# The fifth of seven inner products of an MLP's second layer is multiplied by the seven-product scheme once more

## The chip, the core and the metric

The kernel runs on one core of a Trainium2 chip. The metric is the device time of one execution in microseconds (us). The core has TensorE (PE in the profile; its weight loads are PEld), VectorE (DVE), ScalarE (ACT), GpSimd (POOL) and SyncE (SP), which here issues nearly all DMAs. The 16 DMA engines of the core carry every transfer.

## What is computed

One layer of an encoder trunk on one sequence of 2048 rows and 1024 columns: a mixer (two kinds of attention) and then an MLP, both behind a norm with shift and scale. Only the MLP matters here:

```python
h = rmsnorm(x, g_norm2[l]) * (1.0 + sc2) + sh2
x = x + gt2 * (jnp.square(jax.nn.relu(h @ w1[l])) @ w2[l])
```

`w1` is 1024 x 4096 and `w2` 4096 x 1024, all in float32.

## The kernel before

**Three matmuls for one.** Every float32 operand is split into a rounded part and a rest (`split`: ACT casts `hi`, DVE subtracts to get `lo`). `mm3` then makes three matmuls: hi by hi, hi by lo, lo by hi. Each operand of 128 x 512 so costs one ACT cast and one DVE subtraction, and lies in a tile of the pool `opp`, which has eight.

**Seven products for eight.** Both layers of the MLP are cut in 2 x 2 blocks and multiplied by a Strassen scheme in Winograd's form, which needs seven block products (numbered 1 to 7, `OUTER`) in place of eight, for sums and differences of blocks. Each of the seven takes sums of the blocks of one side and of the other. `mb` is the half of the sequence (mb=1 is worked on first, then mb=0), `tb` a block of 512 rows of it, and `odd` says which of the two.

**The first layer** (class `First`) runs 16 groups of seven steps for each half; a step is 12 matmuls. Its outcome, the hidden activations and their sums, goes to DRAM (`scr_hid[mb, i, ...]`, i being the product of the second layer that will use it).

**The second layer** has the same seven products i, of [hidden, 4096 deep] by [w2]. They come in two kinds.
- A *plain* product (class `Second`, list `PLAIN`) runs 16 steps of 12 matmuls, once for each half of the sequence.
- A *doubled* product (class `Outer`, list `DOUBLE`) takes both halves of the sequence as a 2 x 2 block problem again and applies the seven products inside it: seven times eight steps of 6 matmuls, run once, when mb=0's hidden activations are there. It needs sums on both sides: those of the weights are made ahead, during mb=0's first layer (`outer_sums`, one per group of seven steps, stored to `scr_t`); those of the hidden activations are partly made on the fly, where the first layer subtracts the other half's value from what it stores (`First.other` loads it, `First.keep` subtracts), and partly just before the product, as half sums of 128 x 1024 on DVE (`half`, `half_sum`, placed by `plan`).

Before, the products 1, 6 and 5 are plain and 7, 2, 3 and 4 doubled. The order of work is: out projection, first layer of mb=1, plain 1, 6, 5 of mb=1, first layer of mb=0, plain 1, doubled 7, plain 6, doubled 2, plain 5, doubled 3, doubled 4. Within the plain products of mb=1 lies the preparation of mb=0's normed input (`right_blocks`, four times, ten steps apart). The products 1 and 6 (and 5) are summed in four accumulator tiles (`Second.whole`), and `update` adds these sums to rows of x: it loads a row block, adds (`weigh`, DVE), and stores. A doubled product adds its results itself (`load_x` loads the rows, `end` adds).

**Who sets the order.** The MLP is a list `steps`; `at(n, job)` hangs loads and sums on a step. PE and SP keep the order in which the program emits their instructions; ACT and DVE get theirs from the scheduler of the tile framework. Operands are prepared ahead as long as at most eight tiles are ready or in use; a first-layer step uses one, a plain step two, two doubled steps three. A store that waits for DVE holds up all that SP has behind it; a load also waits until its tile is free.

**The pools.** `ring` (three buffers of 8 KB a partition) and `spare` (one) hold the raw weights; `tp` has seven temporary rows of 128 x 512, `accp` twelve such tiles ("kept"), `rp` two, which hold the norm rows that `right_blocks` multiplies by.

Every group of the profile names line 42, a helper that records instructions, so groups are told apart by their tiles: `opr` and `ol` are the two operands of a doubled product, `oph` and `opv` those of a plain one, `opw` and `h` those of the first layer; `r` is a half of hidden activations, `l` and `hw` raw operands, `xo` and `xu` rows to be added to, `wt` raw weights for sums.

## Time and profile before

| | us |
|---|---|
| median of 3 runs | 2551.41 (2550.36 to 2551.88) |
| profiled execution | 2549.72 |
| its span | 2548.0 |
| PE busy | 2520.9 |
| DVE busy | 2010.0 |
| ACT busy | 1498.6 |
| share of the DMA engines of queue q1 | 79.7% |

The span is the time from the first to the last instruction of the profiled execution. Busy times are unions of an engine's instructions. Matmuls overlap their neighbours, so that an unbroken run of them shows as 100% busy; how many of them fit in a stretch tells whether PE ran at its pace.

### The profile page before, as it was taken

To read this page: it belongs to the slowest core of one execution; us is meant where nothing else is said; L and a number is where in the kernel's file an instruction comes from. 1 tells how busy PE (TensorE), PEld (TensorE's weight loads), DVE (VectorE), ACT (ScalarE), POOL (GpSimd) and SP (SyncE) were. 2 spreads that over 40 slices of the span, in tenths; PEclk is the share of its full clock that TensorE was granted. 3 is DMA by queue.
4 is the path that set the end of the run, shared out by engine and by line. 5 is a ranking of instruction groups with operands and counts; after the bars stand their busy time and mean duration, and the time that the engine had idled before them with its cause. 6 is when DMAs were issued, how large, how long until landed. Compare 5 with 4: busy or idle time off the path is not lost.

```text
span 2548.0 us, 39355 instructions
## 1 busy us (share of the span) xinstructions
PE 2520.9 (99%) x12436; PEld 2104.0 (83%) x12436; DVE 2010.0 (79%) x3509; ACT 1498.6 (59%) x2871; POOL 747.0 (29%) x1128
## 2 busy tenths in 40 slices
PE   9999999999999999999999999999999999999999
PEld 7888888888888888887988888888888887888887
DVE  7656767887789878998858777668988766988897
ACT  6333425668866677666755555566555555656565
POOL 4330154776776667776620000000000000000000
PEclk9999999999999999999999999999999999999999
DMA  9879979779987788866787888787899889777772
GB/s 359 327 295 365 348 269 295 216 243 291 284 237 235 239 251 269 268 211 196 230 301 253 301 284 281 257 312 260 279 323 303 264 274 394 273 285 271 281 266 83
DMA packets 293200, 698.92 MB, mean 274 GB/s; under 512 B 31360, under 2 KB 83584, under 8 KB 281856
## 3 DMA queue, kind: packets, MB, share of 16 engines
q1 hardware_dynamic: 291696, 691.69, 79.7%
q10 hardware_dynamic: 1296, 4.72, 0.5%
q8 instruction: 98, 1.61, 0.3%
q14 instruction: 110, 0.90, 0.1%
HBM read 477.66 MB, written 218.63 MB: 273 GB/s over the span
## 4 chain that ended last, share of the span: by engine, by line
PE 83%; DVE 6%; DMA 3%; ACT 3%; issue 2%; POOL 1%; SPq 0%; DVEq 0%; ACTq 0%; POOLq 0%
PE ps L42 27%; PE ps_s L42 14%; PE pt L42 11%; PE acc L42 6%; PE wt L42 6%; PE pf L42 4%; PE z L42 4%; PE po L42 4%; PE pq L42 3%; DVE p L42 2%; PE cz L42 2%; DMA hw<-in_w_dram 1%; PE ct L42 1%; DVE opr L42 1%; ACT z L42 1%
## 5 line engine op out<-in xcount | busy, mean ns | idle before, releaser
L42 PE MATMUL ps<-h,opw 128*128 128x512 f32 x1512 | 358.6, 389 | 0.0
L42 ACT CAST wth<-wt 128x512 fp32r<-128x512 f32 (+3 forms) x544 | 257.3, 484 | 166.0 <-PE wt L42 156.9
L42 POOL TENSOR_TENSOR b<-p 128x512 f32<-128x512 f32 (+1 forms) x320 | 292.5, 914 | 168.0 <-DVE p L42 95.0
L42 DVE TENSOR_TENSOR wtl<-wt,wth 128x512 fp32r<-128x512 f32 (+3 forms) x544 | 291.2, 547 | 57.6 <-ACT wth L42 55.8
L42 PEld LDWEIGHTS ps<-h,opw 128*128 128x128 f32 x1512 | 283.7, 188 | 58.8
L42 PE MATMUL pt<-w,ht 128*128 128x512 f32 x1248 | 288.2, 391 | 0.0
L42 PE MATMUL ps_s<-h,opw 128*128 128x512 f32 x1152 | 277.3, 389 | 0.4 <-ACT ps_s L42 0.4
L42 PEld LDWEIGHTS pt<-w,ht 128*128 128x128 f32 x1248 | 232.9, 188 | 47.7
L42 DVE TENSOR_TENSOR_SCAN p<-z,p,zero 128x512 f32<-128x512 f32 x192 | 245.8, 1281 | 25.7 <-ACT z L42 18.1
L42 PE MATMUL ps<-oph,opv 128*128 128x512 f32 x1152 | 263.2, 390 | 1.2 <-ACT opv L42 1.1
L42 PEld LDWEIGHTS ps<-oph,opv 128*128 128x128 f32 x1152 | 216.0, 188 | 47.8 <-ACT opv L42 1.9
L42 PEld LDWEIGHTS ps_s<-h,opw 128*128 128x128 f32 x1152 | 215.9, 188 | 46.0 <-ACT ps_s L42 0.8
L42 PE MATMUL acc<-wth,v 128*128 128x512 f32 (+3 forms) x544 | 220.6, 410 | 0.0
L42 ACT CAST opr<-r 128x512 fp32r<-128x512 f32 x224 | 139.7, 625 | 105.5 <-PE ps L42 50.6
L42 ACT ACTIVATE z<-z 128x512 f32<-128x512 f32 (+1 forms) x320 | 166.4, 520 | 55.3 <-PE z L42 48.9
L42 PE MATMUL z<-k,q 128*128 128x512 f32 (+3 forms) x640 | 185.7, 372 | 7.7 <-DVE p L42 7.0
L42 PE MATMUL acc<-wtl,v 128*128 128x512 f32 (+3 forms) x544 | 185.5, 347 | 0.0
L42 PE MATMUL ps<-opr,ol 128*128 128x512 f32 x768 | 176.4, 389 | 0.1
L42 PE MATMUL wt<-ident,b 128*128 128x128 f32 x1088 | 171.4, 273 | 0.9 <-DVE p L42 0.6
L42 DVE TENSOR_TENSOR opr<-r,opr 128x512 fp32r<-128x512 f32 x224 | 151.3, 689 | 25.9 <-ACT opr L42 23.3
L42 PEld LDWEIGHTS wt<-ident,b 128*128 128x128 f32 x1088 | 136.4, 141 | 41.4 <-DVE wtl L42 1.9
L42 PEld LDWEIGHTS ps<-opr,ol 128*128 128x128 f32 x768 | 144.0, 188 | 30.5 <-DVE ol L42 0.4
(214 smaller groups left out, 4846.9 us busy)
## 6 DMA issues: line engine op xcount, KB each, us to landing
q<-scr_q SPq DMA_DIRECT2D x128, 256.0 KB, 5.5
w<-in_w_dram SPq DMA_DIRECT2D x64, 512.0 KB, 5.5
r<-scr_hid SPq DMA_DIRECT2D x64, 512.0 KB, 8.0
k<-scr_k SPq DMA_DIRECT2D x240, 128.0 KB, 4.5
v<-scr_v SPq DMA_DIRECT2D x120, 256.0 KB, 4.2
wa<-in_w_ada_dram SPq DMA_DIRECT2D x48, 512.0 KB, 6.2
ow<-scr_wo SPq DMA_DIRECT2D x24, 1024.0 KB, 6.2
hw<-scr_hid SPq DMA_DIRECT2D x48, 512.0 KB, 6.4
```

The costliest lines, as they stand in the source:

```text
L42: return lambda *x, **y: self.tc.keep_in_program_order(f(*x, **y))
```

## The change

Product 5 moves from the plain list to the doubled one, and stands between 7 and 2 there. So plain 5 of both halves is gone (2 x 16 steps), and a doubled product of 56 steps comes in. The order after mb=0's first layer is then: plain 1, doubled 7, plain 6, doubled 5, 2, 3, 4. What goes with it:

- The first layer of mb=0 makes the difference for product 5 too (`other(5)`): one more load in each of its first eight groups, in one of the two tiles of `rp`, which are free once the norm rows have been used.
- The weight sums of product 5 take product 2's place in the first layer of mb=0, loaded from the sums in `scr_s`. Product 2's weight sums are made in the second half of that layer by `narrow_sums`: eight times two loads of 128 x 512 into temporary rows, four sums of 128 x 256, four stores.
- mb=1's sum of products 1 and 6 is now added by `update` to three more row blocks in the second half of mb=0's first layer, in `rp`'s tiles, one row in four steps; before, this and plain 5 were added during and after mb=1's plain 5. mb=1's accumulator tiles stay in use until then.
- mb=0's updates move into the doubled products 2 (eight rows) and 3 (four rows). Product 5 adds its own results to eight row blocks, as 7 does.
- `right_blocks` of mb=0 now come seven steps apart, in temporary and kept tiles by turns.
- `plan` places the loads and half sums of hidden activations later, and for products 2 and 3 within the product itself, since no plain product stands before them.

```diff
-    PLAIN = (1, 6, 5)
-    DOUBLE = (7, 2, 3, 4)
+    PLAIN = (1, 6)
+    DOUBLE = (7, 5, 2, 3, 4)
...
             def other(self, i):
-                o = First.others[self.mb, self.j, i] = temp(f"o{self.nm}_{i}")
+                nm = f"o{self.nm}_{i}"
+                o = First.others[self.mb, self.j, i] = rp.tile([P, TB], F32, tag="r", name=nm) if i == 5 else temp(nm)
...
-                if i == 5:
-                    column_sum(dve, d["s", n], ps, d["s", n], ALU.add)
...
-            if i == 5:
-                update(mb, 1, 1, spread(1, 2, 3, 9), spread(6, 7, 8, 13))
...
+        def narrow_sums(i, k, step):
+
+            t = []
+            r, s = {2: (0, 1), 4: (1, 1)}[i]
+
+            def load():
+                for a in range(2):
+                    t.append(temp(f"wn{i}_{k}_{a}"))
+                    sp.dma_start(t[a], w2[2 * (HP * a + k) + s][:, r * TB : (r + 1) * TB])
+
+            def sums(pr, dst, a, b, op):
+                v = {nm: t[h][:, c * CN : (c + 1) * CN] for nm, h, c in (("11", 0, 0), ("12", 1, 0), ("21", 0, 1), ("22", 1, 1))}
+                column_sum(dve, v[dst], v[a], v[b], op)
+                later.add(2, lambda: sp.dma_start(scr_t[i, pr][:, k, :], v[dst]))
+
+            at(step - 4, load)
...
-                if i in (3, 7):
+                if i in (3, 7, 5):
...
-                home = kept if self.i == 7 and b in ("22", "11") else temp
+                home = kept if self.i in (5, 7) and b in ("22", "11") else temp
...
-                    outer_sums(DOUBLE[j // 4], j % 4, begin + 7 * j + 5)
+                    outer_sums((7, 5, 3, 4)[j // 4], j % 4, begin + 7 * j + 5)
                     if j < HP:
-                        for i, n in ((3, 2), (2, 5), (7, 2), (4, 5)):
+                        for i, n in ((3, 2), (2, 5), (7, 2), (4, 5), (5, 3)):
                             at(begin + 7 * j + n, lambda i=i, f=f: f.other(i))
+                    else:
+                        narrow_sums(2, j - HP, begin + 65 + 6 * (j - HP))
...
-                    begins = end + 1 + 10 * k
-                    pieces = right_blocks(0, k, temp)
+                    begins = end + 7 * k
+                    pieces = right_blocks(0, k, kept if k % 2 else temp)
...
+                rest = len(steps)
+                lent = lambda nm: rp.tile([P, TB], F32, tag="r", name=nm)
+                for n, (r, odd) in enumerate(((0, 0), (1, 1), (1, 0))):
+                    at_row = rest + 61 + 16 * n
+                    update(1, r, odd, range(at_row, at_row + 16, 4), range(at_row + 4, at_row + 20, 4), lent)
...
-        plan = {"load": {1: (f - 5, 1), 5: (f - 1, 1), 3: (f + 4, 2), 2: (f + 18, 2)}}
-        plan["sum"] = {6: (f + 9, 2), 7: (f + 13, 2), 4: (f + 44, 2)}
-        for i, p in ((7, 6), (2, 5), (3, None), (4, None)):
+        plan = {"load": {1: (f - 3, 1), 5: (f + 2, 2), 3: (f + 10, 2), 2: (f + 18, 2)}}
+        plan["sum"] = {6: (f + 16, 2), 7: (f + 21, 2), 4: (f + 44, 2)}
+        for i in DOUBLE:
             f = outer(i, plan)
             e = len(steps)
-            if p:
-                plain_loads(plain(0, p), [12, 11, 11, 11, 9, 8])
-            plan = {"load": {1: (f + 6, 2), 5: (f + 17, 2), 3: (f + 30, 2), 2: (f + 46, 2)}}
-            plan["sum"] = {6: (e + 1 if i == 7 else f + 38, 2), 7: (e + 4, 2), 4: (e + 8, 2)}
+            if i == 7:
+                plain_loads(plain(0, 6), [12, 11, 11, 11, 9, 8])
+            spread = lambda *ns: [f + n for n in ns]
+            if i == 2:
+                update(0, 0, 0, spread(6, 10, 14, 18), spread(12, 16, 20, 24))
+                update(0, 1, 1, spread(31, 35, 39, 43), spread(36, 40, 44, 48))
+            if i == 3:
+                update(0, 1, 0, spread(12, 16, 20, 24), spread(17, 21, 25, 29), None, True)
+            plan = {"load": {1: (f + 14, 2), 5: (f + 17, 2), 3: (f + 30, 2), 2: (f + 46, 2)}}
+            plan["sum"] = {6: ({7: e + 1, 5: e - 4}.get(i, f + 38), 2), 7: (e + 8, 2), 4: (e + 16, 2)}
```

More of the change, by code (lines that the diff above doesn't have):

```diff
@@ L1697, in outer_sums @@
             at(step - 6, load)
+            todo = ((5, "22", "21", "22", ALU.add), (7, "21", "11", "21", ALU.subtract))
+            todo += ((6, "11", "22", "11", ALU.subtract), (3, "12", "12", "11", ALU.subtract))
+            for n, x in enumerate(todo):
+                at(step + n, lambda x=x: sums(*x))
+        def narrow_sums(i, k, step):
[10 more added lines that the diff above has]
+            at(step - 4, load)
             todo = ((5, "22", "21", "22", ALU.add), (7, "21", "11", "21", ALU.subtract))
@@ L1719, in load @@
                 a, h = {1: (0, 0), 2: (1, 0), 4: (1, 1)}[pr]
-                if i in (3, 7):
+                if i in (3, 7, 5):
                     for m in range(HP // 2):
@@ L1766, in load_x @@
             def load_x(self, b):
-                home = kept if self.i == 7 and b in ("22", "11") else temp
+                home = kept if self.i in (5, 7) and b in ("22", "11") else temp
                 for n in range(2):
                     Outer.outs[b, n] = []
-                    for r, odd in {2: ((0, 1),), 3: ((0, 0),), 4: ((1, 1),), 7: ((1, 1), (1, 0))}[self.i]:
+                    for r, odd in {2: ((0, 1),), 3: ((0, 0),), 4: ((1, 1),), 7: ((1, 1), (1, 0)), 5: ((0, 0), (1, 0))}[self.i]:
                         mb, row = 2 - int(b[1]), HK * r + 2 * (int(b[0]) - 1) + n
@@ L1773, in load_x @@
                         sp.dma_start(x, scr_x[2 * mb + odd, row])
-                        Outer.outs[b, n].append((x, mb, row, odd, self.i != 7 or (mb and not odd)))
+                        Outer.outs[b, n].append((x, mb, row, odd, self.i in (2, 3, 4) or (self.i == 5 and mb and r)))
         halves = {}
```

14 lines of the change are left out of this document (1 added, 13 removed).

## The prediction

> **What bounds the kernel now.** I read the page first, then busy times by stretch, then the chain of waits around the weakest place.
>
> ```profile
> span 2548.0 us, 39355 instructions
> PE 2520.9 (99%) x12436; PEld 2104.0 (83%) x12436; DVE 2010.0 (79%) x3509; ACT 1498.6 (59%) x2871; POOL 747.0 (29%) x1128
> ```
>
> PE is busy 99% of the span. The profiled execution took 2549.72 us, 1.7 us more than its span and 1.7 us less than the median of the runs (2551.41). I sum against the former and add the difference to the median.
>
> Busy time of each engine by stretch (PE, PEld, DVE, ACT, POOL, clock, DMA share, GB/s). I cut where matmuls change their tiles: mb=1's plain products 1, 6, 5; the first half of mb=0's first product; (its second half is left out here); mb=0's plain 1; product 7; plain 6; product 2; plain 5; product 3; product 4 with the end.
>
> ```profile
> 1668.00:1711.60 43.60, 43.60 (x194) 36.13 (x193) 31.92 (x52) 27.21 (x49) 0.00 (x0) 1.00 0.80 290
> 1711.60:1755.00 43.40, 43.40 (x193) 35.93 (x193) 36.16 (x60) 29.57 (x52) 0.00 (x0) 1.00 0.69 255
> 1755.00:1798.50 43.50, 43.50 (x194) 36.03 (x193) 40.61 (x67) 26.51 (x47) 0.00 (x0) 1.00 0.83 290
> 1798.50:1951.00 152.50, 152.50 (x674) 126.33 (x673) 127.15 (x203) 80.24 (x142) 0.00 (x0) 1.00 0.93 307
> ...
> 2103.50:2149.00 45.50, 44.36 (x193) 35.55 (x192) 26.45 (x40) 20.73 (x38) 0.00 (x0) 1.00 1.04 402
> 2149.00:2226.00 77.00, 76.90 (x338) 62.84 (x337) 74.86 (x115) 51.40 (x88) 0.00 (x0) 1.00 0.80 291
> 2226.00:2270.00 44.00, 43.96 (x194) 36.07 (x193) 39.84 (x54) 18.57 (x32) 0.00 (x0) 1.00 0.75 289
> 2270.00:2346.00 76.00, 76.00 (x337) 62.92 (x336) 66.03 (x102) 50.57 (x86) 0.00 (x0) 1.00 0.72 259
> 2346.00:2390.00 44.00, 44.00 (x196) 36.44 (x195) 34.64 (x49) 18.31 (x32) 0.00 (x0) 1.00 0.79 288
> 2390.00:2466.00 76.00, 76.00 (x337) 62.94 (x336) 70.39 (x109) 50.58 (x86) 0.00 (x0) 1.00 0.80 282
> 2466.00:2548.00 82.00, 77.48 (x338) 62.62 (x336) 67.60 (x101) 46.99 (x80) 0.00 (x0) 1.00 0.37 127
> ```
>
> The clock is whole everywhere. The two engines to watch are DVE (70.39 of 76 us in product 3, 74.86 of 77 in product 7) and the DMA engines, at a share of 0.93 in the first product and 1.04 in plain 1. Product 7 and plain 1 are also where PE loses time. Matmul pace, from the chain of waits:
>
> ```profile
> 1932.37 5.44 PE ps L42 x24
> 2065.88 5.21 PE ps L42 x23
> 2098.66 10.00 DMA hw<-in_w_dram
> 2108.72 8.29 DMA r<-scr_hid
> 2117.03 5.63 DMA hw<-in_w_dram
> 2122.68 7.59 DMA hw<-scr_hid
> 2130.33 6.38 DMA hw<-scr_hid
> 2136.81 0.63 ACT oph L42
> 2138.81 11.41 PE ps L42 x49
> ```
>
> 5.44 us / 24 = 0.2267 us a matmul (the 389 ns of the groups is a pipelined latency). So 193 matmuls are 43.75 us, and plain 1 took 45.50: 1.7 us lost. The rows from 2098.66 on say to what: from there to 2138 the chain is DMA alone. Loads of plain 1 land just when their operand is wanted; no slack is left.
>
> **The change, part by part.**
>
> *Matmuls.* Plain 5 ran for both halves: 2 x 16 steps x 12 = 384. Doubled it is 7 x 8 steps x 6 = 336. 48 fewer x 0.2267 = **-10.9 us**, all on the path.
>
> *DVE in the doubled products.* Issued back to back, DVE's instructions stand closer than their mean durations:
>
> ```profile
> 2397.92 0.69 DVE L42 TENSOR_TENSOR opr<-r,opr 128x512 fp32r<-128x512 f32 x1
> 2398.52 0.70 DVE L42 TENSOR_TENSOR ol<-l,ol 128x512 fp32r<-128x512 f32 x1
> 2399.12 0.76 DVE L42 SCALAR_TENSOR_TENSOR txu<-cs,mod,txu 128x512 f32<-128x512 f32 x1
> 2399.78 0.69 DVE L42 TENSOR_TENSOR opr<-r,opr 128x512 fp32r<-128x512 f32 x1
> ...
> 2487.67 1.22 DVE L42 TENSOR_TENSOR r<-r,r 128x1024 f32<-128x1024 f32 x1
> 2488.80 1.29 DVE L42 TENSOR_TENSOR opr<-r,opr 128x512 fp32r<-128x512 f32 x2
> 2490.01 0.69 DVE L42 TENSOR_TENSOR ol<-l,ol 128x512 fp32r<-128x512 f32 x1
> ```
>
> Starts give 0.60 us for a 512-wide operation, 0.66 for a weighted add, 1.13 for a half sum (1024 wide). A doubled product gives it 336 x 0.2267 = 76.2 us. Counted in the changed program's order, from what the first step of one product needs to what the next one's needs (512-wide + half sums + weighted adds):
> - product 7: 84 + 12 + 20 = 50.4 + 13.6 + 13.2 = 77.2 (before 84 + 10 + 20 = 74.9);
> - product 5: 88 + 5 + 20 = 71.7;
> - product 2: 84 + 16 + 22 = 50.4 + 18.1 + 14.5 = 83.0 (before 88 + 5 + 10 = 65.1);
> - product 3: 84 + 12 + 16 = 74.5 (before 88 + 5 + 19 = 71.0);
> - product 4: 82 + 8 + 14 = 67.5, as before.
>
> Product 2 takes in eight update adds and, as no plain product stands between 5, 2 and 3, half sums that plain stretches covered before (products 2's and 3's own). Product 7 before, at 74.9, lost 77.00 - 338 x 0.2267 = 0.4 us: the count is a fair measure. Slack is what operands lie ready: eight tiles, three per two steps of 1.36 us, so at most 7 us, some 3 us after product 5's last adds. Product 2 wants 6.8 us more than PE gives: bounds 6.8 - 7 = 0 and 6.8 with the lead already gone; I take 5.5. Product 3 has 1.7 us to spare but begins without lead, and its eight half sums come in a bunch: 0 to 4, I take 2. Product 7 is 1 us over, with half sums moved into it: 0 to 3, I take 1. Together **+8.5** (0 to 13.8).
>
> *The first product of mb=0, second half.* From its step 61 to its end (51 steps x 2.72 = 139 us) come the narrow sums (16 loads of 256 KB, 32 stores of 128 KB: 8.4 MB) and the twelve rows of mb=1's update (loaded and stored: 6.3 MB). What DMA does there now, and the most it does for long:
>
> ```profile
> 1960.00:2100.00 140.00, 140.00 (x620) 115.95 (x619) 96.12 (x153) 74.88 (x132) 0.00 (x0) 1.00 0.81 270
> 2100.00:2170.00 70.00, 68.86 (x300) 55.84 (x299) 47.82 (x72) 37.85 (x68) 0.00 (x0) 1.00 1.04 392
> ```
>
> 0.270 x 139 + 14.7 = 52.2 MB, which is 376 GB/s. At 392 GB/s that takes 133 us and fits; at the mixed rate of the first half, 307 / 0.93 = 330, it takes 158, 19 us over. Between them, at 361: 145, 6 us over. PE does not feel this inside the first product (one tile a step, eight ready: 8 x 2.72 = 21.8 us of lead at most), but plain 1, which follows, has no slack: every microsecond that its loads come later is one of PE's. Its own moved loads (product 7's halves, later by 2 to 6 steps) take a little from the same crowd: 0 to 2 us gained, I take none.
>
> The rule that speaks most against this: the Trainium skill, "DMA: Bandwidth & Descriptors", section "Where 436 GB/s comes from", lets the HBM side bind at some 358 GB/s a core for transfers between HBM and SBUF. By it these 52.2 MB take 146 us, an estimate of 7 us over, and the sum would come to 2558. The trace shows 392 GB/s over 70 us, so the figure is no ceiling here.
>
> *Lent rows.* The update's rows use the norm rows' two buffers at one row in four steps (10.9 us), each loaded, four steps later added, three later stored. So a load waits on SP for a store issued just before it to land, and all loads behind it wait too. The nearest rows (issue to landing; SP's own waits: total, times, longest; four issues in a row):
>
> ```profile
> scr_x<-txu SPq DMA_DIRECT2D x20, 256.0 KB, 4.2
> ```
>
> ```profile
> SPq L42 <- DMA scr_t<-wt: 50.0, 22, 6.0
> ```
>
> ```profile
> 1790.98 1.85 SPq L42 DMA_DIRECT2D cxu<-scr_x  x4
> ```
>
> Ten such waits, up to 4.2 us each, and 2.3 us each where wide sums wait so today. Where SP would have waited for DVE anyway they cost nothing; else the DMA engines run dry meanwhile. 0 to 10 x 2.3 = 23; as SP has some 26 issues of 1.85 / 4 = 0.46 us in each 19 us (12 us), most are free: I take 2. DMA together **+8** (0 to 42).
>
> *Accumulator rows.* mb=1's four sums now stay in the pool of 12 through the whole first product, so a copy out of PSUM waits for a store of the group before to land. It blocks ACT, which is busy 80.24 of 152.5 us, and is covered by the lead; without that it adds to plain 1's wait, within the bound above.
>
> *mb=1's two plain products* take in the norm work of three: 132 512-wide operations and 4 adds, 82 of 87 us. DVE did 40.61 of 43.5 there without a stall: 0 to 2, I take 0. The product 5 operand (`o5`), its sums from `scr_s` instead of `w2`, and DVE in the first product (371 512-wide operations, 28 of half that width and 11 adds: at most 247 of 305 us) lie under PE: 0.
>
> Sum: -10.9 + 8.5 + 8 = +5.6. 2549.72 + 5.6 = 2555.3, and on the median **2557.0 us**: 0.22% slower, where 0.2% (5.1 us) is about what a measurement of this kernel tells from no change.
>
> **The rivals.**
> - *Faster: the matmuls count and little else.* DMA keeps 392 GB/s (plain 1 waits as today), and DVE's lead carries product 2 but for 3 us, product 3 but for 1: -10.9 + 4 = -7: 2544.5. For it: 2100 to 2170 us at 392 GB/s, and product 7 with 98% of DVE taken losing 0.4 us. Against: that stretch is mostly large loads. It decides if losses stay under 5.8 us in all.
> - *The two cancel.* DVE as summed, DMA 2.5 us: 2551.5.
> - *DMA at the mixed rate.* 330 to 350 GB/s: 10 to 19 us over, less what plain 1 gives back with fewer loads in its second half: -10.9 + 8.5 + 17 = 2566. For it: in 1798 to 1951 a share of 0.93 moves only 307 GB/s, and the added stores are of 1 KB a row. Against: nothing queued up there. By the 358 GB/s of the Trainium skill's page it would not come to this.
> - *The change does nothing:* excluded by the count of matmuls.
>
> **How the numbers follow.** Forecast (both costs) 0.32, with its own range 2552 to 2562, of which 0.04 falls within 0.2%; DMA at the mixed rate 0.20; cancelling 0.28; faster 0.20. So faster 0.20, same 0.32, slower 0.48. The range leaves out the deepest gain (below 2543) and DMA losses of more than 25 us: 2543 to 2575.
>
> **What the profile after would show.** Right: 48 matmuls fewer; PE short of back-to-back in product 2 (4 to 7 us, released by DVE `opr` or `ol`) and product 3, DVE there over 95% busy; DMA share near 1 from 1920 us on, and plain 1 stretched by several us with `hw` loads in its chain. Wrong: product 2 at full pace (DVE count too high), or plain 1 no longer than 45.5 us (DMA is not short). Stalls inside the first product would mean SP's waits are dearer than I took.

## The result, and the profile after

The changed kernel is slower: 2582.31 us in the median of 4 runs (2578.31 to 2583.37) against 2551.64 before, a ratio of 1.0121 with a 95% interval of 1.0108 to 1.0133. That is 30.7 us more, where I forecast 5.6 more and a range that ended at 2575. The profiled execution took 2578.31 us, 28.6 us more than that of before. From the page:

```profile
PE 2527.6 (98%) x12388; PEld 2095.8 (81%) x12388; DVE 2054.9 (80%) x3597; ACT 1510.5 (59%) x2893; POOL 747.6 (29%) x1128
```

PE issues 48 matmuls fewer, as planned, yet is busy longer. Busy times by stage (PE, PEld, DVE, ACT, POOL, clock, DMA share, GB/s; cut where each stage's first matmul starts): mb=1's plain 1 and 6; mb=0's first product in two parts; plain 1; product 7; products 5, 2 and 3 (plain 6, between 7 and 5, is left out).

```profile
1668.88:1712.40 43.52, 43.52 (x193) 36.04 (x192) 33.16 (x54) 29.19 (x51) 0.00 (x0) 1.00 0.84 311
1712.40:1761.27 48.87, 45.91 (x194) 35.53 (x192) 43.48 (x72) 32.34 (x58) 0.00 (x0) 1.00 0.54 192
1761.27:1920.00 158.73, 155.77 (x681) 127.40 (x682) 131.89 (x212) 84.75 (x152) 0.00 (x0) 1.00 0.88 294
1920.00:2082.10 162.10, 153.80 (x666) 125.20 (x664) 122.01 (x209) 75.76 (x135) 0.00 (x0) 0.99 0.97 331
2082.10:2135.44 53.34, 46.89 (x193) 36.64 (x192) 26.56 (x43) 23.58 (x43) 0.00 (x0) 0.97 1.00 374
2135.44:2214.44 79.00, 78.34 (x337) 62.44 (x336) 77.46 (x116) 50.97 (x88) 0.00 (x0) 1.00 0.82 309
...
2258.30:2334.46 76.16, 76.16 (x337) 63.06 (x336) 72.36 (x113) 50.56 (x86) 0.00 (x0) 1.00 0.75 271
2334.46:2415.85 81.39, 79.31 (x338) 62.13 (x336) 81.23 (x120) 50.49 (x86) 0.00 (x0) 1.00 0.83 286
2415.85:2494.69 78.84, 77.87 (x338) 62.61 (x336) 76.65 (x115) 50.56 (x86) 0.00 (x0) 1.00 0.85 301
```

A stage's loss is its length less its matmuls at 0.2267 us: 192 for a plain product (43.5 us), 336 for a doubled one (76.2), 1344 for a first product (304.7). Against before:

| stage | loss before | loss after | more | forecast |
|---|---|---|---|---|
| plain 6 of mb=1 | 0.0 | 5.3 | 5.3 | 0 |
| first product of mb=0, steps 0 to 3 | 0.0 | 2.9 | 2.9 | 0 |
| first product of mb=0, the rest | 0.0 | 13.3 | 13.3 | 0 |
| plain 1 of mb=0 | 2.3 | 9.8 | 7.5 | 8 |
| products 7, 2, 3 | 0.8, 0, 0 | 2.8, 5.2, 2.7 | 2.0, 5.2, 2.7 | 1, 5.5, 2 |

These add up to 38.9; less the matmuls' 10.9 that is 28.0 of the 28.6 us, and 0.5 us more lie ahead of these stages. The doubled products and plain 1 lose what I forecast. In plain 1 it is late loads, as forecast: this is what ACT waits for there (total, times, longest), before and after.

```profile
ACT oph L42 <- DMA hw<-scr_hid: 19.6, 5, 6.6
```

```profile
ACT oph L42 <- DMA hw<-scr_hid: 32.7, 7, 7.9
```

Some 1.6 us of plain 1's loss are its lower clock (0.97 over 53.34 us; see the last section). The surprise stands in the first product and just before it. What PE waits for inside the first product, from 1920 to 2082 us, and what ACT waits for there:

```profile
PE ps_s L42 <- ACT cp L42: 7.2, 5, 4.5
PE ps_s L42 <- DVE cp L42: 1.1, 1, 1.1
```

```profile
ACT cp L42 <- DMA scr_hid<-ca: 21.4, 4, 8.2
ACT cp L42 <- DVE cp L42: 11.1, 8, 3.1
```

Before 1920 us two short waits for DVE's `cp` come on top (0.8 us). So from step 4 on there are eight stops of 9.1 us in all; each costs some 0.3 us more until the matmuls run at their pace again, and a lowered clock behind the longest makes 1.7 us (last section). That is nearly all of the 13.3 us. The longest wait, at one moment: the timelines of PE, of ACT and of SP's issues, and a row of the chain of waits (start, us, what):

```profile
2026.72 2.88 PE L42 MATMUL ps<-h,opw 128*128 128x512 f32 x12
2034.12 4.61 PE L42 MATMUL ps_s<-h,opw 128*128 128x512 f32 x12 [4.51 <-ACT cp L42]
```

```profile
2024.69 0.62 ACT L42 CAST opw<-ts 128x512 fp32r<-128x512 f32 x1
2033.48 0.59 ACT L42 COPY cp<-ps_s 128x512 f32<-128x512 f32 x1 [8.17 <-DMA scr_hid<-ca]
```

```profile
2018.49 0.46 SPq L42 DMA_DIRECT2D scr_t<-twn  x1
2022.58 0.32 SPq L42 DMA_DIRECT2D xu<-scr_x  x1
...
2028.48 0.33 SPq L42 DMA_DIRECT2D scr_hid<-ca  x1
```

```profile
2017.81 4.75 DMA scr_x<-xu
```

Read from below: SP issues nothing from 2018.95 to 2022.58, while a lent row's store lands and frees its tile. A store of `ca` from the group before, which stands behind ten other issues, is so issued only at 2028.48. ACT's copy of product 6's sum out of PSUM takes that tile; it has waited 8.17 us for the store when it starts at 2033.48. PE waits 4.51 us for the copy, because the inner products 6, 7 and 4 write the same PSUM bank (`HOME`): between product 6 and product 7 lies one step, 2.72 us. This wait knows nothing of the eight operand tiles; the operands of the steps there lay ready 16 us ahead in the median and 11 at the least (by the trace, from the end of DVE's subtraction to the step's first matmul).

### The profile page after: what moved, and what is told of

Its sections match the earlier page's. It is cut to its first block, busy times and chain, and to the rows that moved or that the text cites. A ratio compares the mean times of both kernels' runs of the same rounds, so it can differ in the third digit from the quotient of the medians.

```text
span 2576.6 us, 39474 instructions
## 1 busy us (share of the span) xinstructions
PE 2527.6 (98%) x12388; PEld 2095.8 (81%) x12388; DVE 2054.9 (80%) x3597; ACT 1510.5 (59%) x2893; POOL 747.6 (29%) x1128
## 4 chain that ended last, share of the span: by engine, by line
PE 68%; DVE 14%; DMA 9%; ACT 4%; issue 3%; POOL 1%; SPq 1%; DVEq 0%; ACTq 0%; POOLq 0%
PE ps L42 16%; PE ps_s L42 11%; PE pt L42 11%; PE acc L42 6%; PE wt L42 6%; PE pf L42 4%; PE z L42 4%; PE po L42 4%; PE pq L42 3%; DVE opr L42 3%; DVE p L42 2%; DVE r L42 2%; PE cz L42 1%; DMA scr_t<-wt 1%; DVE ol L42 1%
## 5 line engine op out<-in xcount | busy, mean ns | idle before, releaser
L42 PE MATMUL ps_s<-h,opw 128*128 128x512 f32 x1152 | 280.2, 392 | 11.6 <-ACT cp L42 7.5
L42 ACT CAST opr<-r 128x512 fp32r<-128x512 f32 x280 | 174.6, 624 | 138.2 <-PE ps L42 71.6
L42 PE MATMUL ps<-opr,ol 128*128 128x512 f32 x960 | 224.7, 392 | 2.1 <-DVE opr L42 1.7
L42 PEld LDWEIGHTS ps<-opr,ol 128*128 128x128 f32 x960 | 178.9, 188 | 45.5 <-DVE opr L42 6.2
L42 DVE TENSOR_TENSOR opr<-r,opr 128x512 fp32r<-128x512 f32 x280 | 186.3, 689 | 15.2 <-ACT opr L42 13.9
L42 PE MATMUL ps<-oph,opv 128*128 128x512 f32 x768 | 180.5, 394 | 9.3 <-ACT opv L42 8.8
L42 PEld LDWEIGHTS ps<-oph,opv 128*128 128x128 f32 x768 | 144.3, 189 | 45.0 <-ACT opv L42 11.7
L42 PE MATMUL ps_s<-opr,ol 128*128 128x512 f32 x720 | 169.0, 391 | 2.0 <-DVE opr L42 1.6
```

The source lines that it names most:

```text
L42: return lambda *x, **y: self.tc.keep_in_program_order(f(*x, **y))
```

## The experiments

Losses by stage are worked out from each kernel's own trace as above ("start" is steps 0 to 3 of mb=0's first product, "rest" what follows in it); they are us of PE's time. Each row is one profiled execution, which can lie some us from the median (e3_pool_rows: 2569.8 us, the fastest of its four).

| kernel | median us | ratio to before (95%) | plain 6 | start | rest | plain 1 | 7 | 5 | 2 | 3 |
|---|---|---|---|---|---|---|---|---|---|---|
| changed | 2582.3 | 1.0108 to 1.0133 | 5.3 | 2.9 | 13.3 | 9.8 | 2.8 | 0 | 5.2 | 2.7 |
| e1_free_sums | 2581.6 | 1.0107 to 1.0137 | 5.3 | 4.5 | 15.8 | 8.7 | 2.8 | 0 | 5.2 | 2.6 |
| e2_no_rows | 2565.7 | 1.0042 to 1.0072 | 5.3 | 2.9 | 1.9 | 4.8 | 2.8 | 0 | 5.2 | 2.6 |
| e3_pool_rows | 2577.6 | 1.0075 to 1.0114 | 5.3 | 2.9 | 8.2 | 7.9 | 2.8 | 0 | 5.2 | 2.7 |
| e4_no_narrow | 2561.5 | 1.0025 to 1.0051 | 5.3 | 2.9 | 4.2 | 2.8 | 2.8 | 0 | 5.3 | 2.7 |
| e7_narrow_f1 | 2560.8 | 1.0023 to 1.0052 | 6.7 | 4.5 | 1.4 | 2.4 | 2.8 | 0 | 5.2 | 2.7 |
| e6_blocks9 | 2579.8 | 1.0088 to 1.0122 | 0.4 | 7.6 | 16.8 | 9.9 | 2.8 | 0 | 5.2 | 2.7 |
| e8_blocks8 | 2579.2 | 1.0093 to 1.0123 | 6.1 | 0 | 13.7 | 9.8 | 2.8 | 0 | 5.2 | 2.7 |
| e11_pool_mult | 2587.4 | 1.0132 to 1.0162 | 9.7 | 2.3 | 17.2 | 10.1 | 2.8 | 0 | 5.2 | 2.6 |
| e13_split | 2575.3 | 1.0080 to 1.0108 | 1.3 | 0.1 | 16.5 | 9.9 | 2.8 | 0 | 5.2 | 2.7 |
| e5_level | 2585.3 | 1.0112 to 1.0142 | 5.3 | 4.5 | 16.6 | 8.7 | 2.8 | 3.1 | 3.5 | 2.7 |
| e9_level2 | 2579.8 | 1.0101 to 1.0131 | 5.3 | 2.8 | 14.0 | 8.6 | 2.8 | 0 | 4.7 | 2.6 |
| e10_rows_late | 2580.3 | 1.0103 to 1.0133 | 5.3 | 4.5 | 20.9 | 8.9 | 2.8 | 0 | 3.2 | 1.8 |
| e12_pool_halves | 2648.4 | 1.0371 to 1.0402 | 5.3 | 2.8 | 15.7 | 7.6 | 30.0 | 12.5 | 20.1 | 14.3 |
| v1_all | 2557.9 | 1.0018 to 1.0039 | 3.8 | 0.8 | 4.6 | 3.2 | 2.8 | 0 | 4.7 | 2.7 |
| v2_all | 2635.9 | 1.0315 to 1.0350 | 9.7 | 2.2 | 3.7 | 2.5 | 30.6 | 12.8 | 21.3 | 12.7 |
| v3_all | 2548.3 | 0.9981 to 0.9999 | 1.3 | 0 | 3.6 | 2.7 | 2.8 | 0 | 2.3 | 1.0 |

In the kernels that leave the first product as the changed kernel has it (e5, e6, e8 to e13), "rest" came out between 13.7 and 20.9, and 13.3 in the changed kernel's own profiled execution, the fastest of its four. Much of this spread is the granted clock: without what is lost at half clock (1.7 us in the changed kernel, 6.8 in e10_rows_late) all of them lie between 11.6 and 14.0. So differences of a few microseconds there are not read, and small effects are read from the other columns.

### Which part makes the copy late: the held tiles, SP's queue or the bytes

e1_free_sums leaves the additions out, so the tiles are free:

```diff
-                weigh(x, Second.whole["s", n], row)
+                if home is None:
+                    weigh(x, Second.whole["s", n], row)
```

> The changed kernel, with mb=1's sums not added to the twelve late row blocks: the rows are loaded and stored as before, but the four accumulator tiles are free once plain 6 of mb=1 is done. In the changed kernel PE loses 16.2 us in mb=0's first product, and it is released by ACT's copy `cp`, which waits for stores of the group before to land. Theory H (the four held tiles make the copy wait for its tile): without them the copy waits for no store, the loss in the first product falls from 16.2 us to 3 to 6 us (what is left stands at its beginning and in waits for DVE), and the time falls by 10 to 13 us to some 2570 us. Theory Q (the lent rows' blocks on SP's queue make everything late, the copy too): the DMAs are unchanged, so the loss stays at 14 to 16 us and the time within 2 us of the changed kernel's 2582 us.

Measured: 2581.6 us, nothing gained. The copy no longer waits for a store, but now DVE waits for late loads, and PE for DVE's sums out of the same bank. DVE's and PE's waits of e1_free_sums, 1920 to 2082 us:

```profile
DVE ts L42 <- DMA w<-in_w_dram: 12.3, 4, 4.8
...
DVE twn L42 <- DMA twn<-in_w_dram: 6.0, 3, 2.2
```

```profile
PE ps_s L42 <- DVE cp L42: 6.1, 3, 4.8
PE ps L42 <- ACT cp L42: 2.5, 1, 2.5
```

b1_hold is the reverse, the kernel before with the four tiles held:

```diff
+                for n in range(HK):
+                    at(len(steps) + 97 + 4 * n, lambda n=n: hold(n))
```

> The kernel before with one part of the change alone: four operations on DVE read mb=1's four sums late in mb=0's first product, so that four of the twelve accumulator tiles stay held until then; nothing else is changed, no DMA is added. Theory H: the copies wait for stores in the kernel before too, as its SP queue is also behind at times: the first product loses 3 to 10 us where it lost none, and the time is 3 to 10 us over before. Theory Q: without added DMAs SP issues the stores in time, the loss is under 1 us and the time the same.

Measured: 2550.76 against 2550.71 us (ratio 0.9990 to 1.0009), and no loss in the first product. Theory H falls: the held tiles only choose which wait shows the lateness.

e2_no_rows leaves out the rows' transfers (`fetch` returns, `add` only reads the sum):

> The changed kernel, with the twelve late row blocks neither loaded nor stored; an operation of the same length on DVE reads the sums at the same steps, so that the four accumulator tiles stay held as long. Twelve loads and twelve stores of 256 KB are gone, and SP's waits for them. Theory H: a copy still waits for the store of the group before, which is issued a little sooner: the loss in the first product falls by a third at most, from 16.2 us to 10 to 14 us. Theory Q: it falls to 3 to 6 us as the store is no longer queued behind waits. In both, plain 1 gets its loads sooner as 6.3 MB are gone: its loss falls from 9.8 us to 3 to 7 us. Time: 2570 to 2575 us by H, 2563 to 2568 by Q.

Measured: 2565.7 us, "rest" 1.9, as theory Q forecast. This looked like theory Q, but it takes away bytes as well as waits. e3_pool_rows keeps the bytes and takes SP's waits away; e4_no_narrow keeps the rows on SP and leaves out the narrow sums:

```diff
-                sp.dma_start(x, scr_x[2 * mb + odd, HK * r + n])
+                (pool if home else sp).dma_start(x, scr_x[2 * mb + odd, HK * r + n])
...
-                later.add(3, lambda: sp.dma_start(dst, x))
+                later.add(3, lambda: (pool if home else sp).dma_start(dst, x))
```

> The changed kernel, with the loads and stores of the twelve lent rows issued by POOL, which has nothing to do then, in place of SP: the same 24 transfers, but SP no longer waits for a row's store to land before it issues what stands behind. Theory Q (SP's blocked queue): mb=0's first product loses 4 to 6 us in place of 16.2, as it did with the rows left out (4.8), of which 3.0 at its start; plain 1 still pays for the volume and loses 7 to 10 us (9.8 in the changed kernel, 4.8 with the rows left out). Time about 2571 us. Theory V (it was the 6.3 MB, not the queue): the first product keeps a loss of 12 to 16 us, and the time stays at 2578 to 2583 us.

> The changed kernel without the narrow sums: their 16 loads, 32 operations on DVE and 32 stores (8.4 MB) are left out, and product 2 takes product 7's weight sums instead. The lent rows stay on SP. Theory Q (the rows block SP whatever else is moved): the first product still loses 10 to 16 us. Theory V (too many bytes): it loses 4 to 7 us, as with the rows left out. In both, plain 1 gets its loads sooner: 9.8 us of loss falls to 3 to 6 us. Time: 2571 to 2577 us by Q, 2564 to 2568 us by V.

The end of the first product in e2_no_rows, e3_pool_rows and e4_no_narrow, one row of each:

```profile
1920.00:2071.00 151.00, 149.62 (x661) 123.56 (x660) 122.65 (x213) 78.57 (x140) 0.00 (x0) 1.00 0.96 322
```

```profile
1920.00:2076.00 156.00, 151.92 (x664) 123.87 (x663) 121.71 (x208) 76.00 (x136) 12.18 (x22) 1.00 1.01 347
```

```profile
1920.00:2068.50 148.50, 147.35 (x650) 121.36 (x649) 112.66 (x179) 77.45 (x138) 0.00 (x0) 1.00 0.93 314
```

With SP freed of the rows' waits (e3) the DMA engines have a share of 1.01 and the time falls by 4.8 us in the median, with intervals that touch; the first product loses 11.1 us, between what Q and V forecast. With the rows' waits left and 8.4 MB fewer (e4) the time falls by 20.8 us. SP's waits for the rows' stores are even longer in e4 than in the changed kernel (the changed kernel to 2082 us, e4_no_narrow to 2069):

```profile
SPq L42 <- DMA scr_x<-xu: 16.1, 8, 3.4
```

```profile
SPq L42 <- DMA scr_x<-xu: 24.3, 8, 5.3
```

So the bytes decide, and Q is a small part. The narrow sums also take 48 issues off SP, but in the changed kernel SP issues in only 91 of these 162 us. Per megabyte left out the gains agree: 20.8 / 8.4 = 2.5 us, and 16.6 / 6.3 = 2.6 in e2, where a megabyte takes 1 / 0.331 = 3.0 us at the rate of that stretch. Neither part costs so much alone: e2, with only the narrow sums, loses 1.9 and 4.8 us, and e4, with only the rows, 4.2 and 2.8. An estimate says why: at the 347 / 1.01 = 344 GB/s of e3's row, the 139 us that I had counted carry 47.8 MB, of which before took 37.5. The 8.4 MB fit beside these, and so do the 6.3 MB; both together are 4.4 MB too many, or 13 us.

e7_narrow_f1 moves the same 8.4 MB to mb=1's first product:

```diff
                     second_sums(j, begin + 7 * j + 2)
+                    if j < HP:
+                        narrow_sums(2, j, begin + 76 + 5 * j)
```

> The changed kernel with the narrow sums moved, complete, from the second half of mb=0's first product to the second half of mb=1's (where the DMA engines have a share of 0.80 and PE some 17 us of operands ahead). Theory V (the second half of mb=0's first product has more bytes than the DMA engines carry there): the same gain as from leaving them out, the first product's loss falls to about 7 us and plain 1's to about 2.8, time 2561 to 2565 us; mb=1's first product loses under 1 us more. Theory C (the bytes cost wherever they are): mb=1's first product or its plain 1 loses 5 us or more, and the time is 2570 us or more.

Measured: 2560.8 us, as good as leaving them out (2561.5). In the new place the DMA engines are as full, and PE has no stop there (plain 6 and start, behind it, lose 3.0 us more). Late in mb=1's first product, and the old place:

```profile
1600.00:1668.00 68.00, 68.00 (x301) 56.31 (x300) 50.02 (x89) 35.87 (x63) 0.00 (x0) 1.00 1.01 348
1920.00:2068.50 148.50, 148.22 (x654) 122.39 (x653) 112.40 (x178) 78.45 (x139) 0.00 (x0) 1.00 0.93 317
```

That speaks for theory V: it is the same bytes, and only the place differs. A full share alone is no loss. The lead in operands is not the difference (17 us in the median there, 16 in the old place); the new place has no rows to carry beside the narrow sums.

### The normed blocks seven steps apart

b2_blocks7 puts this part alone into the kernel before:

```diff
-                    begins = end + 1 + 10 * k
-                    pieces = right_blocks(0, k, temp)
+                    begins = end + 7 * k
+                    pieces = right_blocks(0, k, kept if k % 2 else temp)
```

> The kernel before with another part of the change alone: the four blocks of normed input are prepared seven steps apart in temporary and kept tiles by turns, so within mb=1's plain 1 and 6 as in the changed kernel. There PE loses 5.3 us in plain 6 of mb=1 and 3.0 us in the first steps after it; before, neither. Theory S (seven steps are too few for one block's chain of ACT and DVE operations beside a plain product's operands): plain 6 loses 4 to 6 us here too, nothing is lost later as plain 5 has room, and the time is 4 to 6 us over before. Rival U (the loss comes from what surrounds plain 6 in the changed kernel: SP held up by a row's store until the first product has begun): plain 6 loses under 1 us here.

Measured: 2557.5 us, 6.8 more than before (ratio 1.0017 to 1.0039); plain 6 loses 5.2 us, as theory S has it, and plain 5 behind it 2.1, which S had at nothing. So the blocks' place does it. Whether by DVE's amount of work or by the chain within a block, four kernels ask. Two spread the blocks (`end - 5 + 9 * k` and `end - 5 + 8 * k`):

> The changed kernel with mb=0's four blocks of normed input begun five steps before mb=1's plain 1 and nine steps apart, in place of seven apart from its start. DVE's work goes from 37.4 and 44.9 us in plain 1 and 6 of mb=1 to 40.5 and 38.9 us, where PE takes 43.5 for each. Theory S (blocks seven steps apart are too close): plain 6 loses 0 to 1 us in place of 5.3 and the first steps behind it 0 to 1 us in place of 3.0, so the time is 6 to 8 us less, 2574 to 2576 us. Rival U (the loss comes from a chain within one block, however far apart): 3 to 5 us stay in plain 6, and the time is 0 to 3 us less.

> The changed kernel with the four blocks of normed input begun five steps before mb=1's plain 1 and eight steps apart, so that the last ends at step 28 of 32; seven apart from the start it ended at 30, and nine apart (begun five steps earlier) at 31, where plain 6 lost 0.4 us, but the first steps of the first product 8.0 in place of 3.0. Theory S' (both ends count: the blocks need room between them, and the last must be done before the first product begins): plain 6 and the first three steps behind it lose 0 to 3 us together in place of 8.4, and the time is 5 to 8 us less than the changed kernel's, 2574 to 2577 us. Rival U (what is lost is only moved about): 6 to 8 us stay, and the time is within 2 us of 2582.

Both missed: plain 6 and start together lost 8.0 and 6.1 us against 8.2; the loss moved between them. e11_pool_mult gives sixteen of DVE's operations to POOL:

> The changed kernel with sixteen of the operations that prepare mb=0's normed blocks (the products with the norm rows, 0.60 us each on DVE, 9.6 us in all) on POOL, which is idle there, in place of DVE; the blocks stay seven steps apart. DVE's work in mb=1's two plain products falls from 82.4 to 72.8 us of 87. Theory E (DVE's excess in plain 6, 44.9 us of work in 43.5, is what the squeezed blocks cost): plain 6 and the first three steps behind it lose 0 to 3 us in place of 8.4. Rival U (the chain of ACT and DVE in one block): they lose 5 us or more, as the chain is as long. Rival P (POOL and DVE disturb each other at the same memory port): DVE's operations there take clearly longer than 0.69 us on average and the loss stays or grows.

Measured: 2587.4 us, worse, by rival P (below): DVE's subtractions for `opv` in plain 6 take 903 ns in the mean in place of 684. e13_split keeps every operation; it moves ACT's casts one step behind the differences they read and begins the blocks one step earlier:

```diff
+            def sums():
+                low(1, "11")
+                low(3, "22")
+                less("11", "12", "11")
+                low(2, "21")
+                less("12", "22", "12")
+
+            def highs():
+                high(5, "11")
+                high(7, "12")
...
-                    begins = end + 7 * k
+                    begins = end - 1 + 7 * k
```

> The changed kernel with each block of normed input cut finer: where ACT's cast of a difference stood in the same job as DVE's subtraction that makes it, it now stands one step (2.72 us) later, and the blocks begin one step earlier, still seven apart. Number, kind and engine of the operations are the same. In the changed kernel ACT is busy 62 of 94 us in mb=1's two plain products and waits for DVE's differences for 26 more, with the operands' casts queued behind. Theory A (ACT, in order, is blocked by the chain within a block): its waits for DVE fall under 10 us and plain 6 with the three steps behind it loses 0 to 3 us in place of 8.4. Theory E (DVE's work, 44.9 us in plain 6 of 43.5, is the limit): it still loses 5 us or more.

Measured: 2575.3 us, 7.0 less than the changed kernel; plain 6 and start lose 1.4 us in place of 8.2. ACT's waits for DVE during mb=1's plain products, in the kernel before (three of them, 130.6 us), in the changed kernel (two, 92.4 us) and in e13_split (two, 88.3 us):

```profile
ACT h L42 <- DVE ty L42: 24.7, 16, 2.9
```

```profile
ACT h L42 <- DVE ty L42: 12.7, 8, 2.9
ACT h L42 <- DVE cy L42: 9.7, 6, 3.3
```

```profile
ACT h L42 <- DVE ty L42: 7.5, 8, 2.2
...
ACT h L42 <- DVE cy L42: 5.6, 4, 2.9
```

The waits were there before too; the change packs them closer. In the changed kernel ACT is busy 29.2 + 32.3 us (rows above) and waits 22.4: 84 of 92.4 us, with the operands' casts queued behind each wait. Cutting 22.4 to 13.1, less than theory A asked for, was enough. DVE does nearly as much in plain 6 as in the changed kernel (70 operations and 42.23 us there, for 72 and 43.48), too little of a difference for 6.8 us, so E falls.

### DVE in the doubled products

In the changed kernel 4.3 of product 2's 5.2 us are lost in its steps 20 to 31, where half sums, update adds and operands come together. PE's weight loads wait there for DVE, in the main for `opr` (whole product):

```profile
PEld ps L42 <- DVE opr L42: 3.0, 6, 1.0
PEld ps_s L42 <- DVE opr L42: 2.9, 5, 1.4
```

Three experiments move this work. e5_level moves four update rows and four half sums from product 2 to product 5; e9_level2 moves update rows of product 2 to 3 and of 3 to 4; e10_rows_late does that and takes the remaining rows of products 2 and 3 to steps 36 to 48, away from the half sums:

```diff
-                update(0, 0, 0, spread(6, 10, 14, 18), spread(12, 16, 20, 24))
-                update(0, 1, 1, spread(31, 35, 39, 43), spread(36, 40, 44, 48))
+                update(0, 0, 0, spread(31, 35, 39, 43), spread(36, 40, 44, 48))
             if i == 3:
+                update(0, 1, 1, spread(31, 35, 39, 43), spread(36, 40, 44, 48))
```

> The changed kernel with DVE's work levelled between products 5 and 2: four update rows of mb=0 are added in product 5 in place of product 2, and product 2's first four half sums are made at step 38 of product 5 in place of step 52 on. By instructions, product 5 goes from 72.0 to 79.2 us and product 2 from 83.4 to 76.2, where PE takes 76.2 for each. Theory D (what DVE has to do above PE's pace is what is lost): product 5 begins with some 5 us of operands ahead and loses 0 to 2 us, product 2 loses 1 to 3 us in place of 5.2, so the time is 2 to 4 us less, 2578 to 2580 us. Rival L (product 2's loss comes from loads of hidden halves or weight sums that are late): product 2 still loses 4 to 5 us.

> The changed kernel with four update rows of mb=0 added in product 3 in place of product 2, and the four that were in product 3 in product 4: by instructions DVE has 80.8 us of work in product 2 (83.4 in the changed kernel), 74.9 in product 3 as before and 70.5 in product 4 (67.9), where PE takes 76.2. Theory D (the excess of DVE's work over PE's pace is lost): product 2 loses 2 to 4 us in place of 5.2, products 3 and 4 what they lost, time 1 to 3 us less. Rival B (half sums that come four in a row are what stalls, whatever the total): product 2 keeps 4.5 us or more.

> The changed kernel with the update rows of mb=0 one product later, as in the experiment with 80.8 us of DVE work in product 2, and besides, product 2's four remaining update adds at its steps 36 to 48 in place of 12 to 24, so that they no longer fall among the four half sums at steps 16 to 22 (and product 3's likewise). DVE's totals are those of that experiment, which lost 4.7 us in product 2. Theory B (what stalls is the local crowd at steps 20 to 29: four half sums of 1.13 us, adds and operands in 11 us): product 2 loses 1 to 3 us and product 3 0.5 to 2 (2.7 before), time 3 to 5 us under the changed kernel's. Theory D (the total of DVE's work in a product): 4 to 5 us stay in product 2, time as in that experiment, 2578 to 2581 us.

Measured by stage, as the times are swamped by "rest". Product 2 in e9_level2 and in e10_rows_late:

```profile
2334.37:2415.27 80.90, 78.88 (x338) 62.36 (x337) 80.05 (x118) 50.41 (x86) 0.00 (x0) 1.00 0.80 284
```

```profile
2341.74:2421.07 79.33, 78.64 (x337) 62.28 (x336) 78.63 (x116) 50.40 (x86) 0.00 (x0) 1.00 0.79 278
```

Levelling products 5 and 2 lost 3.1 + 3.5 in place of 5.2: worse. With 2.6 us of work fewer, product 2 lost only 0.5 us less than in the changed kernel (e9, as rival B has it); with the same work as e9 and the adds moved off the half sums 2.0 less (e10). Product 4 paid 1.3 us for it in each. So both count, and the crowd counts for more than the total; of e10's forecast of 1 to 3 us, 3.2 is just outside.

e12_pool_halves gives the half sums to POOL (`column_sum(pool, ...)` in `half_sum`):

> The changed kernel with all half sums of hidden activations (128 x 1024) on POOL in place of DVE, which then has 13.6, 5.7, 18.1, 13.6 and 9 us less to do in products 7, 5, 2, 3 and 4. Theory D/B (DVE's excess in the doubled products, in total or locally): products 7, 2 and 3 lose 0 to 1 us each in place of 2.8, 5.2 and 2.7, time 7 to 10 us under the changed kernel's. Rival P (POOL and DVE disturb each other): DVE's operations in product 2 get longer (0.69 us on average now) and the loss falls by less than half, or a half sum takes so long on POOL (over 2.5 us) that operands come late.

Measured: 2648.4 us, 66 worse than the changed kernel. Timelines of e12_pool_halves in product 7, POOL and DVE:

```profile
2137.28 19.52 POOL L42 TENSOR_TENSOR r<-r,r 128x1024 f32<-128x1024 f32 x7
```

```profile
2140.61 2.85 DVE L42 TENSOR_TENSOR ol<-l,ol 128x512 fp32r<-128x512 f32 x1
2143.39 5.65 DVE L42 TENSOR_TENSOR opr<-r,opr 128x512 fp32r<-128x512 f32 x2
```

A half sum takes 2.79 us on POOL, and beside it each of DVE's subtractions lasts 2.8 us in place of 0.69: one of DVE's for one of POOL's.

### All together

> The changed kernel with all together: narrow sums in mb=1's first product, lent rows issued by POOL, blocks begun four steps earlier and eight apart, update rows of products 2 and 3 one product later. If the four causes add (DMA in the first product 20 us, blocks 8, DVE in product 2 some 2.5), the first product loses 2 to 4 us, plain 1 about 2.8, plain 6 of mb=1 0 to 2, product 2 about 3, and the time is 2548 to 2554 us: level with the kernel before or a little under it. If the causes share one bottleneck, it stays above 2560 us.

Measured: 2557.9 us, between the two forecasts. DMA's part is mended ("rest" 4.6, plain 1 3.2), but spacing the blocks was no cure (3.8 and 0.8 us stay), and the rows one product later take 0.5 us off product 2 and put 1.9 on product 4.

> The changed kernel with the narrow sums in mb=1's first product, the lent rows issued by POOL, and both the norm products and the half sums on POOL. If POOL is a free engine (no rival P): the first product loses 2 to 4 us, plain 1 2.4 to 3.2, plain 6 of mb=1 0 to 2, the doubled products 0 to 2 in all: 2542 to 2549 us, faster than the kernel before. If rival P holds: 2552 to 2562 us, as with the moves alone (2557.9).

Measured: 2635.9 us, by rival P, and worse than that rival's forecast: DMA's part is mended ("rest" 3.7, plain 1 2.5), the doubled products are not.

> The changed kernel with what the runs point to: narrow sums in mb=1's first product, blocks cut finer as in e13_split, update rows of mb=0 one product later and at steps 36 to 48, and the half sums of product 4's inner block four steps apart from step 18 in place of two from step 16. POOL is given nothing. If e13_split's theory A holds and the crowds in the doubled products thin out (product 2 loses 1.5 to 3 us, product 3 0.5 to 1.5), what is lost over the kernel before is 8 to 12 us against 10.9 us of matmuls: 2547 to 2552 us, level with the kernel before or up to 0.15% faster. If theory E holds: 2554 to 2558 us.

v3_all takes the cures that held: narrow sums 5 steps apart from step 72 of mb=1's first product, e13_split's blocks, rows at steps 36 to 48 one product later, and

```diff
-            plan["sum"] = {6: (...), 7: (e + 8, 2), 4: (e + 16, 2)}
+            plan["sum"] = {6: (...), 7: (e + 8, 2), 4: (e + 18, 4)}
```

Measured: 2548.3 us (11 runs) against 2550.92, a ratio of 0.9981 to 0.9999, as forecast: 34 us under the changed kernel and a hair under the kernel before. Its busy times, the second half of the first product, plain 1 and product 2:

```profile
1920.00:2066.37 146.37, 145.83 (x642) 120.12 (x641) 110.12 (x174) 76.62 (x135) 0.00 (x0) 1.00 0.91 310
2066.37:2112.55 46.18, 44.70 (x194) 35.85 (x193) 23.61 (x38) 20.98 (x38) 0.00 (x0) 1.00 1.03 388
2311.53:2389.94 78.41, 77.54 (x338) 62.48 (x336) 78.41 (x116) 50.44 (x86) 0.00 (x0) 1.00 0.81 281
```

In product 2 nothing is lost at steps 20 to 31 any more; 1.9 of its 2.3 us stand from step 44 on, where the rows' adds now end. What the doubling saves (10.9 us) and what its company costs still nearly cancel.

## Why the prediction was wrong

- *Matmuls, -10.9 us:* right; 48 fewer, and products without a stall run at 76.16 us.
- *DVE in the doubled products, +8.5:* right in sum and by product: 9.9 (5.2, 2.7 and 2.0 for 5.5, 2 and 1). Its ground was half right. The count by product found the place, but what stalls is the crowd of half sums and adds at steps 20 to 31; a count in windows of eight steps might have shown it.
- *The first product, second half, +6 for DMA:* this is the term that failed, in size and in place. I set 361 GB/s, between 392 and the mixed 330. The stretch ran at 331 GB/s with a share of 0.97: the mixed rate, which I had worked out and given a chance of 0.20. At that rate my own working gives 19 us, and the loss was 13.3 + 7.5 = 20.8. That these agree so well is partly luck: 3.4 of the 20.8 us were lost at half clock, and at a full share this mix ran at 344 GB/s (e3), by which my working gives 13 us; SP's waits seem to make up the rest (e3, without them, loses 8.2 + 5.6, of which 1.7 at half clock). The row with 392 GB/s was of mostly large loads, as I noted; the row of 330 was of the same product's other half, and nearness should have chosen it. By the rule of the Trainium skill that I weighed ("DMA: Bandwidth & Descriptors", "Where 436 GB/s comes from": some 358 GB/s a core) it would have been an estimated 7 us: the measured rate is lower than its figure here and, with 374 GB/s in plain 1, higher there.
- *"PE does not feel this inside the first product":* false. The lead in operands was there, 16 us of it in the median, and PE stopped all the same, for a PSUM bank that ACT's copy or DVE's sum had not left, with one step of cover. A lead counted in one resource covers lateness in that one only.
- *Accumulator rows, covered:* the wait came true (21.4 us of ACT's), but holding them costs nothing by itself (b1_hold) and freeing them gains nothing (e1_free_sums).
- *Lent rows' blocks on SP, +2:* not far off; 4.8 us in the median by e3_pool_rows, hardly told from none. I had written that stops inside the first product would mean SP's waits are dearer; e4_no_narrow, which keeps those waits and even has longer ones, shows that they meant too many bytes.
- *mb=1's two plain products, 0:* the second failure, 8.2 us. I compared DVE's work with the time of both products together (82 of 87 us) and did not look at ACT, which was busy or blocked by DVE for 84 of 92 us. The chain inside a block decided, not the amount.
- *Plain 1, +8 at its door:* right in size, 7.5.

Of the rivals, the mixed rate (2566) was the true one for DMA; with the blocks' 8.2 and the doubled products' 1.4 above my sum it comes to 2575.6. Of the 6.7 us that are missing, 3.8 are DMA's (20.8 for 17) and 2.3 stand between the changed kernel's profiled execution and its median (4.0 where before had 1.7).

## What to carry to other kernels

Cost added transfers at the rate of the nearest crowd in size and mix, not of the fastest stretch, and count whether all that is added to one stretch fits: the same 8.4 MB cost 21 us in one first product, beside 6.3 MB of other added transfers, and no measurable time in the other, which had none. Before calling lateness covered, list every wait of the engine, PSUM banks as well as operands, with the lead of each. For an engine that works in order, count busy time and blocked time together, and separate a producer on one engine from its consumer on the other by a step of other work.

## What the runs showed of the hardware

A stop of PE can be followed by slow matmuls. In the changed kernel, behind the 4.51 us stop shown above, twelve matmuls took 4.61 us where the twelve before the stop took 2.88. By stretch:

```profile
2034.60:2038.00 3.40, 3.40 (x10) 2.65 (x9) 2.23 (x4) 1.76 (x3) 0.00 (x0) 0.50 1.01 333
2038.20:2050.00 11.80, 11.80 (x54) 9.75 (x53) 9.03 (x16) 6.48 (x12) 0.00 (x0) 1.00 0.76 269
```

The granted clock is 0.50 for 3.4 us and then whole again; that is 1.7 us on top of the stop. A stop of 2.1 us at step 2 of the first product, the same in both, was followed by a clock of 0.50 in e1_free_sums and of 1.00 in e2_no_rows. PE's timeline there, then two stretches of 3.4 us, of the one and of the other:

```profile
1768.30 4.61 PE L42 MATMUL ps_s<-h,opw 128*128 128x512 f32 x12 [2.10 <-ACT ps_s L42]
```

```profile
1765.20:1768.60 3.40, 1.30 (x6) 0.79 (x5) 3.25 (x6) 3.40 (x7) 0.00 (x0) 0.99 0.97 355
1768.60:1772.00 3.40, 3.40 (x9) 2.65 (x8) 3.40 (x7) 1.19 (x3) 0.00 (x0) 0.50 0.65 249
```

```profile
1768.84 3.03 PE L42 MATMUL ps_s<-h,opw 128*128 128x512 f32 x12 [2.10 <-ACT ps_s L42]
```

```profile
1764.90:1768.30 3.40, 1.83 (x9) 1.18 (x7) 3.26 (x6) 2.82 (x7) 0.00 (x0) 1.00 0.99 379
1768.30:1771.70 3.40, 2.86 (x12) 2.36 (x13) 3.38 (x6) 2.04 (x5) 0.00 (x0) 1.00 0.92 328
```

That is the difference between 4.5 and 2.9 us in the table's column "start". The stretches lie on a grid of 3.413 us, counted from a change of the clock in the same trace; two falls of the clock in the changed kernel, at 2034.56 and 2109.65 us, lie 22 such steps apart. In e1_free_sums the stop, with 0.65 us lost in step 0 just before, falls into one stretch, in which PE is busy for 1.30 us; in e2_no_rows an edge cuts the stop, and PE is busy for 1.83 us in the first part. All twenty traces fit this from 1500 us on: each of the 49 stretches at full clock with at most 1.43 us of matmuls was followed by half clock, and of the 142 with 1.47 to 2.7 us only four. So the busy time in such a stretch seems to decide; no run varies it by itself, so this is inferred from the traces. The Trainium skill, "TensorE: Matmul & The Clock Gate", Part 1 on the clock gate, has a window of about 3.4 us that runs free of the kernel, after which an idle PE is halved. The length and the free phase agree; that PE must be idle for the window does not, with 1.30 of 3.40 us busy.

POOL is no free help to DVE. Its half sum of 2.79 us held each of DVE's operations with two inputs from SBUF for as long (2.8 us for 0.69), while DVE's adds with one of their two tiles in PSUM kept their time, eight of the 34 wholly beside a half sum of POOL. DVE on `txo<-ps_s`, changed kernel and e12_pool_halves (ns, least, median, most):

```profile
L42 DVE SCALAR_TENSOR_TENSOR txo<-ps_s,mod,txo x34: 740/745/757, 2170.2 to 2572.4; 128x512 f32<-128x512 f32 x34
```

```profile
L42 DVE SCALAR_TENSOR_TENSOR txo<-ps_s,mod,txo x34: 733/740/751, 2185.7 to 2645.9; 128x512 f32<-128x512 f32 x34
```

The Trainium skill, "SBUF — State Buffer", section "Who interferes with whom", says just this: an instruction of VectorE with two inputs from SBUF contends with one of GpSimd that reads SBUF, as an exclusive lock, and one with a single such input (outside its two-port modes) does not. The trace agrees, with these numbers.
